# Column roll of an 8192 x 8192 float32 matrix: heads carried in four stages of 4 rows per partition, where it was two stages of 8 rows

## The chip, the core and the metric

The kernel runs on one core of a Trainium2 chip. The metric is the device time of one execution in microseconds (us), of which a lower one is better. Executions are called fast or slow by their state; all that are used here are fast, at a granted clock of 1.0. The experiments were run in groups, each called a call here; in the six calls, on at least four chips, the same kernel took from 818 to 833 us (817.75 and 821.00 us in two calls on one chip), so a time is only compared with the time of the kernel before in the same call.

A ratio is the mean time of one kernel's fast runs over that of the other's fast runs of the same rounds. It is not quite the ratio of the medians, which are quoted beside it. In the profile's lines DVE is VectorE, POOL the GpSimd engine, SP and ACT the two engines that issue the body copies; q0, q1 and q10 are DMA queues.

## The reference

```python
def setup_inputs():
    return {"x": np.random.randn(8192, 8192).astype(np.float32), "shift": 100}

def reference(x, shift):
    return np.roll(x, shift, axis=1)
```

Each row moves 100 columns to the right, and its last 100 columns come round to the front. Nothing is computed: 268.44 MB are read and 268.44 MB written.

## The kernel before

The output row is cut at column a = 128. The **body**, columns 128 and up, is copied from DRAM to DRAM, one row of 32256 bytes after another, on two hardware queues. The **heads**, columns 0 to 127 of every row, are gathered in SBUF, put together by VectorE, and stored from there by the software queue that POOL feeds. With s = 100 and g = a - s = 28, row r has a head of 100 columns from its own end and 28 columns from its own start. The rows are taken in groups of four (Q = 4). At each of the three borders inside a group, one load takes 128 columns across the border, the last 100 of one row and the first 28 of the next, and VectorE copies each part to its row's head. Only the 100 columns of the fourth row's own end and the 28 of the first row's own start are loaded by themselves.

```python
xm = x.rearrange("(c e j) w -> c j e w", e=16, j=4)
om = out.rearrange("(c e j) w -> c j e w", e=16, j=4)
for c in range(n_rows // 64):                      # the body
    for j in range(4):
        engines[j % 2].dma_start(out=om[c, j, :, a:], in_=xm[c, j, :, g:n_cols - s])
# ...
Q, J = 4, 8                                        # the heads
n_st = n_rows // (P * Q * J)                       # stages
reads = ctx.enter_context(tc.tile_pool(name="reads", bufs=n_st))
heads = ctx.enter_context(tc.tile_pool(name="heads", bufs=n_st))
# ... xt, ot: x and out as "(k p j q) c -> k q p j c"
for k in range(n_st):
    t = reads.tile([P, Q - 1, J, a], x.dtype)
    h = heads.tile([P, Q, J, a], x.dtype)
    for q in range(1, Q):
        lead = bass.AP(tensor=x.tensor, offset=(k * P * J * Q + q) * n_cols - s,
                       ap=[[J * Q * n_cols, P], [Q * n_cols, J], [1, a]])
        nc.gpsimd.dma_start(out=t[:, q - 1], in_=lead)
    nc.gpsimd.dma_start(out=h[:, Q - 1, :, :s], in_=xt[k, Q - 1, :, :, n_cols - s:])
    nc.vector.tensor_copy(h[:, :Q - 1, :, :s], t[:, :, :, :s])
    nc.gpsimd.dma_start(out=h[:, 0, :, s:], in_=xt[k, 0, :, :, :g])
    nc.vector.tensor_copy(h[:, 1:, :, s:], t[:, :, :, s:])
    tiles.append(h)
for k, h in enumerate(tiles):
    for q in range(Q):
        nc.gpsimd.dma_start(out=ot[k, q, :, :, :a], in_=h[:, q])
```

Of the kernel before, what the change touches and what calls it, by code (L numbers as in the profile page):

```python
# [1 line left out]

# [4 lines left out]


@with_exitstack
def kernel(  # L10
    ctx: ExitStack,
    tc: tile.TileContext,
    x: bass.AP,
    shift: int,
    out: bass.AP,
):
    nc = tc.nc
    n_rows, n_cols = x.shape
    s = shift % n_cols
    a = -(-s // 128) * 128  # L20
    g = a - s
    P = nc.NUM_PARTITIONS
    engines = [nc.sync, nc.scalar]
    n_chunks = 16
    rows = n_rows // n_chunks





    xm = x.rearrange("(c e j) w -> c j e w", e=16, j=4)
    om = out.rearrange("(c e j) w -> c j e w", e=16, j=4)
    if a < n_cols:
        for c in range(n_rows // 64):
            for j in range(4):
                engines[j % 2].dma_start(out=om[c, j, :, a:], in_=xm[c, j, :, g:n_cols - s])
    if a == 0:
        return


    if a > 512:
        for i in range(n_chunks):
            r = slice(i * rows, (i + 1) * rows)
            nc.gpsimd.dma_start(out=out[r, :s], in_=x[r, n_cols - s:])
            if g > 0:
                nc.gpsimd.dma_start(out=out[r, s:a], in_=x[r, :g])
        return





    Q, J = 4, 8
    n_st = n_rows // (P * Q * J)
    reads = ctx.enter_context(tc.tile_pool(name="reads", bufs=n_st))
    heads = ctx.enter_context(tc.tile_pool(name="heads", bufs=n_st))
    xt = x.rearrange("(k p j q) c -> k q p j c", q=Q, j=J, p=P)
    ot = out.rearrange("(k p j q) c -> k q p j c", q=Q, j=J, p=P)
    tiles = []
# [9 lines that stand above are left out]
        if g > 0:  # L69
# [8 lines that stand above are left out]
# [1 line left out]
_INS = ['x', 'shift']  # L79
_OUTS = [((8192, 8192), 'float32')]  # L80

_NUMBERS = {'shift': 100}


# [26 lines left out]
```

## Time and profile before

| | before |
|---|---|
| median of the first three runs | 828.16 us (828.02 to 828.73) |
| profiled execution | 826.9 us |
| DMA engines busy | all slices but the last |
| body queues q1 and q10 | 95.0% of the 16 engines' time |
| software queue q0 (heads) | 4.1% |
| heads over at | 252 us |

The page's slices, its queues, the waits of SP and a table by stretches are shown and read in the prediction. One more part of the page matters here, the DMA issues: output and input, issuing engine, number, KB of each, and the median us from issue to landing.

```profile
out_dram<-in_x_dram ACTq DMA_DIRECT2D x256, 504.0 KB, 12.7
out_dram<-in_x_dram SPq DMA_DIRECT2D x256, 504.0 KB, 12.7
out_dram<-h POOLq DMA_DIRECT2D x8, 512.0 KB, 97.6
```

A body copy of the same size as a head store lands in 12.7 us, a store in 97.6. The store isn't slow; it stands behind up to seven others on a queue that gets one small packet for each large one of the body.

### The profile page before, as it was taken

To read this page: it belongs to the slowest core of one execution; us is meant where nothing else is said; L and a number is where in the kernel's file an instruction comes from. 1 tells how busy PE (TensorE), PEld (TensorE's weight loads), DVE (VectorE), ACT (ScalarE), POOL (GpSimd) and SP (SyncE) were. 2 spreads that over 40 slices of the span, in tenths; PEclk is the share of its full clock that TensorE was granted. 3 is DMA by queue.
4 is the path that set the end of the run, shared out by engine and by line. 5 is a ranking of instruction groups with operands and counts; after the bars stand their busy time and mean duration, and the time that the engine had idled before them with its cause. 6 is when DMAs were issued, how large, how long until landed. Compare 5 with 4: busy or idle time off the path is not lost. (4 is left out here: it accounts for less than half of the span.)

```text
span 826.9 us, 589 instructions
## 1 busy us (share of the span) xinstructions
DVE 3.7 (0%) x4; POOL 16.1 (2%) x22
## 2 busy tenths in 40 slices
DVE  0000000000000000000000000000000000000000
POOL 3001001000000000000000000000000000000000
DMA  9999999999999999999999999999999999999997
GB/s 305 336 338 333 337 344 351 347 352 343 339 342 330 329 329 321 334 329 326 326 328 325 337 329 325 340 318 329 317 336 333 330 325 326 328 326 339 321 328 261
DMA packets 18724, 272.70 MB, mean 330 GB/s; under 512 B 8480, under 2 KB 8480, under 8 KB 10528
## 3 DMA queue, kind: packets, MB, share of 16 engines
q10 hardware_dynamic: 8192, 132.14, 47.8%
q1 hardware_dynamic: 8192, 132.14, 47.2%
q0 software_dynamic: 2336, 8.39, 4.1%
q14 instruction: 4, 0.03, 0.0%
HBM read 268.44 MB, written 268.44 MB: 649 GB/s over the span
## 5 line engine op out<-in xcount | busy, mean ns | idle before, releaser
L75 POOL DMA_DIRECT2D out_dram<-h x8 | 6.9, 955 | 92.4 <-DMA h<-in_x_dram 79.9
L66 POOL DMA_DIRECT2D t<-in_x_dram x6 | 5.4, 910 | 0.8 <-PEq L106 0.8
L68 DVE COPY h<-t 128x2400 f32<-128x2400 f32 x2 | 2.8, 1410 | 116.2 <-DMA t<-in_x_dram 116.2
L67 POOL DMA_DIRECT2D h<-in_x_dram x2 | 1.8, 882 | 15.1 <-DMA t<-in_x_dram 15.1
L70 POOL DMA_DIRECT2D h<-in_x_dram x2 | 1.8, 883 | 14.4 <-DMA t<-in_x_dram 14.4
L71 DVE COPY h<-t 128x672 f32<-128x672 f32 x2 | 1.0, 504 | 0.0
L92 POOL MEMSET const-float32-0.0<- 128x1 f32 x1 | 0.1, 98 | 0.2 <-issue 0.2
L92 POOL MEMSET const-bfloat16-1.0<- 128x1 bf16 x1 | 0.1, 101 | 0.0
L92 POOL MEMSET const-float32-1.0<- 128x1 f32 x1 | 0.1, 98 | 0.0
L92 POOL MEMSET const-uint8-127<- 128x1 uint8 x1 | 0.1, 98 | 0.0
## 6 DMA issues: line engine op xcount, KB each, us to landing
out_dram<-in_x_dram ACTq DMA_DIRECT2D x256, 504.0 KB, 12.7
out_dram<-in_x_dram SPq DMA_DIRECT2D x256, 504.0 KB, 12.7
out_dram<-h POOLq DMA_DIRECT2D x8, 512.0 KB, 97.6
t<-in_x_dram POOLq DMA_DIRECT2D x6, 512.0 KB, 65.8
h<-in_x_dram POOLq DMA_DIRECT2D x2, 400.0 KB, 84.0
h<-in_x_dram POOLq DMA_DIRECT2D x2, 112.0 KB, 81.3
```

The costliest lines, as they stand in the source:

```text
L66: nc.gpsimd.dma_start(out=t[:, q - 1], in_=lead)
L67: nc.gpsimd.dma_start(out=h[:, Q - 1, :, :s], in_=xt[k, Q - 1, :, :, n_cols - s:])
L68: nc.vector.tensor_copy(h[:, :Q - 1, :, :s], t[:, :, :, :s])
L70: nc.gpsimd.dma_start(out=h[:, 0, :, s:], in_=xt[k, 0, :, :, :g])
L71: nc.vector.tensor_copy(h[:, 1:, :, s:], t[:, :, :, s:])
L75: nc.gpsimd.dma_start(out=ot[k, q, :, :, :a], in_=h[:, q])
L92: nc = _bacc.Bacc("TRN2", target_bir_lowering=False, num_devices=1)
```

## The change

The intent is to have smaller stages: four instead of two, so that the first stores can start earlier and the transfers are finer. Nothing else is altered.

```diff
-    Q, J = 4, 8
+    Q, J = 4, 4
     n_st = n_rows // (P * Q * J)
```

Through n_st and J this makes 36 head DMAs of half the size out of 18, eight VectorE copies out of four, and a distance of 16 rows (512 KiB) in DRAM from one partition to the next, where it was 32 rows (1 MiB).

## The prediction

> **What bounds the kernel now.** I read the page's slices first, then its DMA queues, then the waits of the SP engine, then a table by stretches of time.
>
> ```profile
> span 826.9 us, 589 instructions
> DVE 3.7 (0%) x4; POOL 16.1 (2%) x22
> ...
> DMA  9999999999999999999999999999999999999997
> ...
> q10 hardware_dynamic: 8192, 132.14, 47.8%
> q1 hardware_dynamic: 8192, 132.14, 47.2%
> q0 software_dynamic: 2336, 8.39, 4.1%
> ...
> HBM read 268.44 MB, written 268.44 MB: 649 GB/s over the span
> ```
>
> The reader should see that no compute engine matters, and that the 16 DMA engines are busy in every slice but the last. The queue shares are time, and 47.8 + 47.2 + 4.1 = 99.1%: the DMA engines are the bound. Two hardware queues carry the body (columns 128 and up, straight from DRAM to DRAM), 264.28 MB; the software queue, fed by POOL, carries the heads (the first 128 output columns, through SBUF), 4.19 MB in and 4.19 MB out. The change touches q0 only.
>
> ```profile
> SPq L36 <- DMA out_dram<-in_x_dram: 679.2, 252, 6.0
> ```
>
> This is the longest wait of the SP sequencer: nearly always it waits for an earlier body copy to land before it may issue the next. So the body is refilled as fast as it drains, and if q0 uses an engine less, the body takes that time at once.
>
> ```profile
> 1.00:131.00 130.00, 3.66 (x4) 12.38 (x14) 1.00 0.99 335
> 131.00:252.00 121.00, 0.00 (x0) 3.47 (x4) 1.00 1.00 346
> 260.00:800.00 540.00, 0.00 (x0) 0.00 (x0) 1.00 1.00 328
> ```
>
> Columns: stretch, length, DVE, POOL, clock, share of the DMA engines, GB/s moved. From the trace's records of single packets, the tenth and last head load lands at 131 us and the eighth and last head store at 252 us; these three stretches are therefore loads, stores, and body alone. The heads are over with 575 us still to run. Nothing that makes the heads later by less than that can delay the end as a wait. They cost time only by the share of the 16 engines that they take.
>
> **What that share costs.** In the packet records body copies move 300.6 GB/s during the loads, 314.3 during the stores, and 328.1 alone. The loss is (328.1 - 300.6) x 131 us = 3.60 MB plus (328.1 - 314.3) x 121 us = 1.67 MB, together 5.27 MB, which at 328.1 GB/s is 16.1 us. This is the price of all the heads in the end time, 1.9% of it: 11.0 us for loads, 5.1 us for stores. It is less than the 33.9 us of q0 (4.1% of the span), because body packets take 1.39 us while loads run and 1.50 us while stores run, and 1.56 us alone; the small packets relieve them. If the heads became free the gain would be 2%, and to lose 2% they would have to double their price.
>
> **What the Trainium skill says.** "DMA: Bandwidth & Descriptors", section "Queues, rings and completion order": each engine goes round robin over the queues that have work, a packet at a time. The trace agrees in pace: a 512 KB store is eight data packets and one completion packet per engine, and eight stores took 121 us, 15.1 us each, so 1.68 us a turn, near one body packet of 1.50 us and one head packet of 0.17 us. Section "SWDGE vs HWDGE vs iDMA" of the same page puts a packet at preferably 4096 bytes and at most 64 descriptors. Here 1792 packets on q0 are 4096 bytes (eight rows of 512), 160 are 4400 (eleven rows of 400) and 32 are 4144 (37 of 112). Eleven and 37 are not multiples of the eight rows of a partition, so packets run across partitions, which the next part uses. Section "Rules for kernel authors" asks for at least 1 MiB a DMA; the trace contradicts that this matters here, since 0.5 MiB transfers with seven more behind them leave the engines at 1.00. Section "Latency and other measured facts" reports lower rates at partition pitches of large powers of two in HBM (207 GB/s at 512 KiB, 164 at 2 MiB); no run here has yet shown that, and it is a rival below.
>
> **The change part by part.** J goes from 8 to 4, so stages from 2 to 4. The SBUF held is the same (four stages of half the size), and so are the bytes and the rows of each descriptor.
> - *DMA instructions.* Loads 10 to 20, stores 8 to 16, each of half the size. POOL spends 0.88 to 0.96 us on each: 36 x 0.9 = 32 us instead of 16. It is spread over some 200 us, in which one DMA drains in about 8 us. Off the path: 0.
> - *Data packets.* A 256 KB transfer gives each engine 32 rows: four packets of eight. Loads of 400-byte rows give 11 + 11 + 10, three packets where 64 rows gave six; loads of 112-byte rows give one where 64 gave two. Sum: 2048 data packets before and after. Their time, 538.9 us in 16 engines, stays. 0.
> - *Completion packets.* One per DMA and engine: 288 becomes 576. The records give each 9 ns: 288 x 9 ns / 16 = 0.16 us. Even with a turn each they yield to the body, which loses nothing by it.
> - *Pace of the heads.* A completion packet takes a turn. Before: loads 6 x 9 + 2 x 7 + 2 x 3 = 74 turns in 131 us (1.77 us each), stores 8 x 9 = 72 in 121. After: loads 12 x 5 + 4 x 4 + 4 x 2 = 84 turns, 149 us; stores 16 x 5 = 80 turns, 134 us. So I expect the last load at about 149 us and the last store at about 283 us instead of 252. It lies beside the body and costs nothing.
> - *Waits for semaphores.* Before, the ninth head DMA was held 15.1 us although its tile was new: it waited for the first of the eight before it. So eight head DMAs may be in flight. After, eight of half the size are 40 turns, 67 us of work: q0 does not run dry. Median store latency should fall from 97.6 to about 67 us.
> - *DVE.* Eight copies instead of four, of half the size; 1410 ns becomes about 750 and 504 about 300. Total from 3.7 to about 4.2 us, off the path.
>
> Sum: +0.2 us on the path, in a kernel whose three runs lie 0.7 us apart.
>
> **Rivals.**
> 1. *Each DMA has a fixed price.* With 18 more at some 2 us of issue and landing each, 36 us would be added, to 864 us. Against: the heads end at 252 of 827 us and DMAs overlap, eight in flight.
> 2. *The software queue does not join the rows of two partitions.* With four rows per partition, packets of 512-byte rows would be 2048 bytes and there would be twice as many. If each costs half, nothing; if each keeps the 0.17 us of a store, 1792 x 0.17 / 16 = 19 us at the very worst of engine time, and about half of it (16.1/33.9) in the end time: 837 us. The 4400-byte packets speak against.
> 3. *The DRAM pitch from partition to partition falls from 1 MiB to 512 KiB.* Loads cost 0.35 us a packet on average where stores cost 0.17, though their lower half, too, takes 0.16: some loads meet congestion. If the new order of addresses removed all of it, loads would cost like stores and (11.0 - 5.1) = 6 us would go, to 822 us. Against: each transfer covers rows four apart without gap in both versions; only how many of them an engine takes in one piece changes. I expect at most 1 us.
> 4. *Completion packets stall an engine until its writes have landed.* 288 more, if each stopped its engine 1 us, would be 18 us, to 846. Against: the body has 8192 of them already and the engines' time is full with data packets.
>
> **Range and chances.** The sum gives 828.2 + 0.2, rival 3 draws a little down: 828.0 us. The range from 823.5 to 831.5 holds the spread of runs, another chip's small difference, most of rival 3 and a third of rival 2. Faster by 2% (under 811.6) needs all the heads free: 0.02. Slower by 2% (over 844.7) needs rival 1 or 4: 0.02. Within 2%: 0.96.
>
> **What would show it.** Right: DMA tenths at 9 up to the last slice; q0 with 2624 packets, 8.39 MB, about 4.1%; q1 and q10 unchanged; 36 head issues with stores landing in about 67 us; heads over at about 283 us; POOL near 32 us; the same 328 GB/s after the heads. Heads over by about 252 would mean that completion packets take no turn. Wrong: q0 with some 4400 packets (rival 2), load packets below 0.25 us on average (rival 3), body packets longer than 1.56 us or engines idle in the early slices (rival 4). A time off by 2% with none of these I could not explain.

## The result, and the profile after

The changed kernel took 832.34 us (median of 6 runs, 829.82 to 835.45), the kernel before 827.84 us (median of 6, 827.28 to 828.73). The ratio is 1.0055, with a 95% interval of 1.0034 to 1.0076. It is the same within 2%, as the prediction said, but 4.5 us slower and 0.8 us outside the stated range, and the interval leaves out 1. The profiled execution is the slowest of the six.

The page of the changed kernel, in the lines that answer to those of before:

```profile
span 833.3 us, 617 instructions
...
DVE 4.5 (1%) x8; POOL 27.2 (3%) x40
...
DMA  9999999999999999999999999999999999999997
...
q1 hardware_dynamic: 8192, 132.14, 47.7%
q10 hardware_dynamic: 8192, 132.14, 47.3%
q0 software_dynamic: 2624, 8.39, 4.0%
...
HBM read 268.44 MB, written 268.44 MB: 644 GB/s over the span
...
out_dram<-h POOLq DMA_DIRECT2D x16, 256.0 KB, 65.4
```

The queues carry the same bytes. q0 has 288 more packets, all of them completions, and no larger share. The engines are as busy as they were. So in this pair of executions nearly all of the additional time is not idle time of the engines: it must be in the duration of packets, and as q0's share did not grow, in those of the body. The wait of SP for body copies shows the same from the issuing side (679.2 us before).

```profile
SPq L36 <- DMA out_dram<-in_x_dram: 685.6, 252, 4.8
```

The table by stretches (stretch, length, DVE, POOL, clock, share of the DMA engines, GB/s), first of the kernel before:

```profile
60.00:125.00 65.00, 1.83 (x2) 3.46 (x4) 1.00 1.00 340
125.00:160.00 35.00, 0.00 (x0) 3.47 (x4) 1.00 1.00 349
160.00:284.00 124.00, 0.00 (x0) 0.00 (x0) 1.00 1.00 340
300.00:800.00 500.00, 0.00 (x0) 0.00 (x0) 1.00 1.00 328
```

and of the changed kernel:

```profile
60.00:125.00 65.00, 2.25 (x4) 6.90 (x9) 1.00 1.01 335
125.00:160.00 35.00, 1.03 (x2) 3.66 (x5) 1.00 1.00 322
160.00:284.00 124.00, 0.00 (x0) 5.68 (x8) 1.00 1.00 338
300.00:800.00 500.00, 0.00 (x0) 0.00 (x0) 1.00 1.00 327
```

The engines are at 1.00 in both, yet while the heads run they move fewer bytes, above all from 125 to 160 us, where loads give way to stores. In the records of single packets, 16 engines spend 786.6 us on the body instead of 780.7 us, and 33.3 us on the heads instead of 33.7. At 300 us the changed kernel is 44 body rows behind, which is 44 / 10.17 rows per us = 4.3 of the 6.4 us by which the two profiled executions differ.

A useful measure of this is the **relief**: how much shorter body packets are while heads run than when the body is alone, times their number, over 16 engines. Before: (1561 - 1443) ns x 2392 / 16 = 17.6 us. After: (1563 - 1489) ns x 2700 / 16 = 12.5 us. What the heads cost is their own 33.7 us less the relief, 16.1 us; in this execution of the changed kernel it is 33.3 - 12.5 = 20.8 us. The heads' own packets hardly changed, and the relief is 5 us smaller. These are two single executions, the second the slowest of six; the repeats further down show less of this.

### The profile page after: what moved, and what is told of

The parts are those of the page before. It is cut to its first block, busy times and chain, and to the rows that moved or that the text cites. A ratio compares the mean times of both kernels' runs of the same rounds, so it can differ in the third digit from the quotient of the medians.

```text
span 833.3 us, 617 instructions
## 1 busy us (share of the span) xinstructions
DVE 4.5 (1%) x8; POOL 27.2 (3%) x40
## 3 DMA queue, kind: packets, MB, share of 16 engines
q0 software_dynamic: 2624, 8.39, 4.0%
## 5 line engine op out<-in xcount | busy, mean ns | idle before, releaser
L75 POOL DMA_DIRECT2D out_dram<-h x16 | 11.6, 724 | 111.8 <-DMA out_dram<-h 59.8
L66 POOL DMA_DIRECT2D t<-in_x_dram x12 | 9.5, 792 | 34.6 <-DMA h<-in_x_dram 17.2
L68 DVE COPY h<-t 128x1200 f32<-128x1200 f32 x4 | 3.1, 786 | 141.6 <-DMA t<-in_x_dram 141.6
L67 POOL DMA_DIRECT2D h<-in_x_dram x4 | 3.0, 748 | 24.9 <-DMA t<-in_x_dram 24.9
L70 POOL DMA_DIRECT2D h<-in_x_dram x4 | 3.0, 748 | 24.0 <-DMA t<-in_x_dram 24.0
L71 DVE COPY h<-t 128x336 f32<-128x336 f32 x4 | 1.7, 425 | 0.0
## 6 DMA issues: line engine op xcount, KB each, us to landing
out_dram<-h POOLq DMA_DIRECT2D x16, 256.0 KB, 65.4
```

## The experiments

All kernels but one give the right result. Each was timed in 4 to 6 fast runs beside 9 to 11 runs of the kernel before in the same call.

### Is it the number of DMAs, their completions, or the order of rows in memory?

The stretches in which body packets grew suggested two theories: A, each further DMA stops its engines for some 0.3 us at its completion, or B, the new layout, four rows per partition, hurts. Cutting every head DMA in two without changing the layout separates them:

```diff
-            nc.gpsimd.dma_start(out=ot[k, q, :, :, :a], in_=h[:, q])
+            for j in (0, 4):
+                nc.gpsimd.dma_start(out=ot[k, q, :, j:j + 4, :a], in_=h[:, q, j:j + 4])
```

(and the loads in the same way).

> Two stages with 8 rows per partition as before, so the rows of DRAM go to the partitions as before, but every head DMA is cut in two over its rows: 36 DMAs, as many as in the changed kernel. Theory A (each further DMA has a price of its own, some 0.3 us per completion packet on each engine: 5.7 us more body packet time over 18 more completions): 832 us, 1.005 of before, heads over at about 284 us. Theory B (the order of the addresses, four rows per partition, costs the time): 828 us, 1.000 of before.

Measured: 819.95 us against 817.98 us before, ratio 1.0022 (1.0008 to 1.0035). It lies between the two expectations and decides nothing by itself. Its heads were over at 281 us, so the number of DMAs sets the pace of the heads whatever the layout is.

The completions by themselves:

```diff
+    pt = pings.tile([1, 144, 128], x.dtype)
+    for i in range(144):
+        nc.gpsimd.dma_start(out=pt[:, i], in_=x[i:i + 1, :128])
```

> The kernel before, with 144 further one-row loads of 512 bytes into a spare tile issued behind the heads, so that they fall into the stretch where the body runs alone. If each puts one completion packet on every engine, 2304 completions are added. Theory A (0.3 us of engine time for each): 144 x 0.3 = 43 us, 871 us. If a completion costs only its 9 ns: 144 x 9 ns = 1.3 us, 829 to 830 us.

Measured: 819.45 us against 817.98, ratio 1.002 (1.0008 to 1.0032): 1.6 us for 144 DMAs, where theory A asked for 43. The page and two stretches of this kernel:

```profile
q0 software_dynamic: 6944, 8.47, 4.4%
...
pt<-in_x_dram POOLq DMA_DIRECT2D x144, 0.5 KB, 24.7
```

```profile
252.00:690.00 438.00, 0.00 (x0) 66.30 (x137) 1.00 1.00 331
690.00:800.00 110.00, 0.00 (x0) 0.00 (x0) 1.00 1.00 333
```

q0 has 4608 packets more than the 2336 of before: on each engine 144 pieces of 32 bytes (a row of 512 bytes was spread over all 16) and 144 completions. The body next to them hardly loses, 331 GB/s against 333. A completion costs no more than about 1.6 us / 144 = 11 ns of engine time (5 to 18 ns by the interval, the piece of 32 bytes included), near the 9 ns that the records give. Theory A's price is excluded, and with it the prediction's rivals 1 and 4; these were loads, and for stores the run with 2 rows below says the same.

Then other sizes of stage, with the diff `Q, J = 4, 16` and `Q, J = 4, 2`.

> One stage with 16 rows per partition: 9 head DMAs instead of 18. Theory A: 9 x 0.3 us less, 825.3 us (0.997). Theory B: some change of either sign from the other address order, and the same number as A only by chance; stores start only when the whole load is done, so there can be a gap in the heads, which costs nothing.

Measured: 819.86 us against 817.98, ratio 1.0019 (1.0005 to 1.0033). Half the DMAs gained nothing.

> Eight stages with 2 rows per partition: 72 head DMAs, 54 more than before, packets still of 8 rows. Theory A: 54 x 0.3 = 16 us more, 844 us (1.020). Theory B: no fixed relation to the number of DMAs; if the step from 8 to 4 rows is the mechanism, one more halving gives perhaps as much again, 837 us (1.011).

Measured: 818.03 us against 817.98, ratio 1.0004 (0.9987 to 1.0021). 54 more DMAs of 128 KB and less cost nothing that these runs can see, and a step further in the direction of the change does not add to its loss. Both theories miss here: there is no rule by which fewer rows per partition are slower.

```profile
out_dram<-h POOLq DMA_DIRECT2D x32, 128.0 KB, 37.0
t<-in_x_dram POOLq DMA_DIRECT2D x24, 128.0 KB, 35.5
```

### Is it there at all?

With three of four kernels at 1.002, only one of them (the 144 small loads) where a completion's own 9 ns would put it, chance became a theory (C). The changed kernel was run twice more, unaltered, with a copy of the kernel before as a control.

> The changed kernel again, unaltered, beside the kernel before on the chip of this call. Theory B (the address order costs engine time): 1.005 of before again. Theory C (the 0.55% was chance: which of several equally good interleavings of the two body queues the runs of that call fell into): between 0.998 and 1.003.

Measured: 821.12 us against 818.13, ratio 1.0035 (1.0018 to 1.0051).

> The kernel before, unaltered, as if it were a new kernel. All theories: 1.000. What it differs from 1.000 by is what two identical programs differ by in this test; theory C expects up to 0.2 or 0.3%.

Measured: 817.43 us against 818.13, ratio 0.999 (0.9975 to 1.0006).

> The changed kernel a second time in the same call. Theory B: the same ratio as the first, near 1.005. Theory C: within 0.3% of 1, and not necessarily the same as the first.

Measured: 820.48 us against 818.13, ratio 1.0031 (1.001 to 1.0051). The loss is there on another chip, a little smaller: 2.7 us by the mean of the two ratios.

The body was run without any heads (a `return` ahead of them; a wrong result):

> The body alone, heads left out on purpose (columns 0 to 127 of the output are not written, so the result is wrong). The prediction's price for all head work, 16.1 us, should be missing: 828 - 16 = 812 us on a chip where before takes 828 us, or 818 - 16 = 802 us on one where it takes 818 us; ratio 0.980. If heads cost their whole engine time of 33.9 us, the ratio would be 0.959.

Measured: 801.7 us against 818.13, ratio 0.9797 (0.9782 to 0.9812), so the heads cost 818.13 x 0.0203 = 16.6 us. The page:

```profile
q10 hardware_dynamic: 8192, 132.14, 49.6%
q1 hardware_dynamic: 8192, 132.14, 49.5%
```

Two queues hold 99.1% of the engines' time, the same sum as three did before. This settles the price on which the prediction's chances rested: half of the heads' own engine time, not all of it.

### A price per transfer, or something that comes once?

If the loads or the stores of the changed kernel are dearer, repeating them makes it larger. The 512-byte loads were repeated four times into spare tiles, behind the stores, with 8 and with 4 rows:

```diff
+    again = ctx.enter_context(tc.tile_pool(name="again", bufs=4 * n_st))
+    for k in [k for _ in range(4) for k in range(n_st)]:
+        u = again.tile([P, Q - 1, J, a], x.dtype)
+        for q in range(1, Q):
+            nc.gpsimd.dma_start(out=u[:, q - 1], in_=lead)   # lead as above
```

> The kernel before with the three 512 KB loads of each stage issued four more times into spare tiles, behind the stores. The prediction priced all loads at 11.0 us, these are three quarters of them: four more sets cost 4 x 8.3 = 33 us, ratio 1.040. All theories say the same; it is the base for its sister with four rows per partition.

Measured: 843.55 us against 817.75, ratio 1.0322 (1.0305 to 1.034): 817.75 x 0.0322 / 4 = 6.6 us a set.

> The same with four rows per partition: four more sets of loads on top of the changed kernel. Theory D (the extra 2.7 us of the change lies in its loads): each set 2.0 us dearer, so 2.7 + 4 x 2.0 = 10.8 us over the sister with eight rows, 1.3% of the time. Theory E (it lies in the stores) or C (it comes once, from how the body queues fall in with the heads, and is not a price per transfer): 2.7 us or less over the sister.

Measured: 848.88 us (843.38 to 849.47) against 817.75, ratio 1.0368 (1.0341 to 1.0395). Over its sister: 817.75 x 0.0046 = 3.8 us, where theory D needed 10.8.

The stores three times more:

```diff
-    for k, h in enumerate(tiles):
+    for k, h in [kh for _ in range(4) for kh in enumerate(tiles)]:
```

> The kernel before with all stores of the heads issued three more times (the same bytes to the same place). The prediction priced all stores at 5.1 us: 3 x 5.1 = 15 us more, ratio 1.019.

Measured: 837.13 us against 817.75, ratio 1.0239 (1.0223 to 1.0255): 817.75 x 0.0239 / 3 = 6.5 us a set.

> The same with four rows per partition. Theory E (the extra 2.7 us of the change lies in its stores): 4 x 2.7 = 10.8 us over the sister with eight rows. Theory D or C: 2.7 us or less over the sister.

Measured: 840.52 us against 817.75, ratio 1.0284 (1.0262 to 1.0306): 817.75 x 0.0045 = 3.7 us over its sister, where theory E needed 10.8.

The loads of 400- and 112-byte rows, the only transfers not repeated so far, were repeated eight times:

```diff
+    for k in [k for _ in range(8) for k in range(n_st)]:
+        u = again.tile([P, J, a], x.dtype)
+        nc.gpsimd.dma_start(out=u[:, :, :s], in_=xt[k, Q - 1, :, :, n_cols - s:])
+        nc.gpsimd.dma_start(out=u[:, :, s:], in_=xt[k, 0, :, :, :g])
```

> The kernel before with the loads of 400- and 112-byte rows of each stage issued eight more times into spare tiles, behind the stores. They are a quarter of the loads by bytes, priced by the prediction at 11.0 x 0.25 = 2.8 us a set: 8 x 2.8 = 22 us more, ratio 1.027. It is the base for its sister.

Measured: 850.02 us against 832.55 (a slower chip), ratio 1.0217 (1.02 to 1.0234): 832.55 x 0.0217 / 8 = 2.3 us a set.

> The same with four rows per partition. Theory F (the 2.7 us or more of the change lie in these small-row loads): 9 x 2.7 = 24 us over the sister with eight rows. Theory C (it comes once, from the way heads and body interleave): 4 us or less over the sister.

Measured: 853.6 us against 832.55, ratio 1.0249 (1.023 to 1.0268): 832.55 x 0.0032 = 2.7 us over its sister, where theory F needed 24.

In all three pairs four rows lose some 3 us, as they do without repetition, although up to nine times the transfers are made. Theories D, E and F fall: the loss doesn't grow in proportion to the transfers. That it comes once, with the heads' first passage, is the reading that is left and is not shown. The spread of these pairs, 2 to 2.6 us with the intervals of both ratios, leaves room for up to about 1 us a set of 512-byte loads or of stores; the middle values are 0.3, 0.3 and 0 us.

### The order inside a stage

Theory C once more, as an accident of which transfers meet: the same transfers with q counted down instead of up, in loads and stores.

```diff
-        for q in range(1, Q):
+        for q in range(Q - 1, 0, -1):
# ...
-        for q in range(Q):
+        for q in range(Q - 1, -1, -1):
```

> The kernel before with the order of its 512-byte loads and of its stores within a stage turned round: the same transfers, the same number, the same bytes. A price of the transfers would give 1.000. Theory C (interleaving): up to 0.4% off, either way.

Measured: 831.26 us against 832.55, ratio 0.9982 (0.9968 to 0.9995).

> The changed kernel with the order turned round in the same way. If four rows per partition have an inherent price in the heads as a whole, 1.003 to 1.005 as before; theory C: anything between 0.999 and 1.005, and a value at 1.000 would speak for it.

Measured: 836.52 us against 832.55, ratio 1.0036 (1.0015 to 1.0056); over its sister 1.0036 / 0.9982 = 1.0054. The loss survives another order. Chance alone is no longer a good explanation: seven comparisons of four rows with eight (1.0055, 1.0035, 1.0031, and over their sisters 1.0045, 1.0044, 1.0031, 1.0054) have one sign, though some share a base. The stretches of the reversed kernels, eight rows first:

```profile
125.00:160.00 35.00, 0.00 (x0) 3.44 (x4) 1.00 1.00 346
160.00:290.00 130.00, 0.00 (x0) 0.00 (x0) 1.00 1.00 340
```

and four rows:

```profile
125.00:160.00 35.00, 1.20 (x2) 3.68 (x5) 1.00 1.01 329
160.00:290.00 130.00, 0.00 (x0) 5.68 (x8) 1.00 1.00 333
```

Again the rate falls from 125 us on, with the engines at 1.00. This led to theory G: the loss arises where head loads and head stores overlap. The repeats of the changed kernel already spoke against it: from 125 to 160 us they moved 343 and 351 GB/s, beside 349 in the copy of the kernel before, and were slower all the same.

### The passage from loads to stores

One kernel was to take the overlap away, by storing the last stage first; the other was to spread it over the heads, by storing each stage after the next one's loads.

```diff
-    for k, h in enumerate(tiles):
+    for k, h in list(enumerate(tiles))[::-1]:
```

> The changed kernel with the stages stored in reverse order, so the first store needs the last load: no head load and head store are in flight together. Theory G (the extra 3 us arise where head loads and head stores overlap, at the passage from one to the other): 1.000 of before, give or take 0.1%, and no stretch of long body packets at 125 to 155 us. If the passage is not the cause: 1.003 to 1.005 as the changed kernel.

Measured: 823.06 us against 821.0, ratio 1.0029 (1.0011 to 1.0047). The separation was only partly reached, as the timeline of POOL and DVE shows (start, us, engine, line, operation):

```profile
118.76 1.49 POOL L75 DMA_DIRECT2D out_dram<-h  x2 [20.44 <-DMA h<-in_x_dram]
142.68 0.79 DVE L68 COPY h<-t 128x1200 f32<-128x1200 f32 x1 [34.61 <-DMA t<-in_x_dram]
143.38 0.33 DVE L71 COPY h<-t 128x336 f32<-128x336 f32 x1
144.00 0.71 POOL L75 DMA_DIRECT2D out_dram<-h  x1 [23.75 <-DVE h L71]
```

Two stores were issued ahead of the last loads, at 118.76 us, against the order of the program; the others waited until 144 us. So two stores still overlapped with loads, where the changed kernel has five by 138 us. The loss stayed about what it was.

```diff
         tiles.append(h)
+        for m in ([k - 1] if k else []) + ([k] if k == n_st - 1 else []):
+            for q in range(Q):
+                nc.gpsimd.dma_start(out=ot[m, q, :, :, :a], in_=tiles[m][:, q])
-    for k, h in enumerate(tiles):
-        for q in range(Q):
-            nc.gpsimd.dma_start(out=ot[k, q, :, :, :a], in_=h[:, q])
```

> The changed kernel with each stage stored as soon as the next one's loads are issued: loads and stores overlap through most of the 280 us of the heads instead of some 25. Theory G: several times the extra, 1.010 or more. If overlap is not the cause: 1.003 to 1.005, or less.

Measured: 823.47 us against 821.0, ratio 1.0035 (1.002 to 1.005). The line of the stores and a piece of the timeline show that they did lie among the loads:

```profile
L75 POOL DMA_DIRECT2D out_dram<-h x16: 709/728/1027, 45.6 to 219.2; - x16
```

```profile
76.61 0.75 POOL L66 DMA_DIRECT2D t<-in_x_dram  x1 [6.93 <-DMA h<-in_x_dram]
79.92 0.75 POOL L67 DMA_DIRECT2D h<-in_x_dram  x1 [2.56 <-DMA h<-in_x_dram]
89.55 0.75 POOL L70 DMA_DIRECT2D h<-in_x_dram  x1 [8.88 <-DMA out_dram<-h]
96.59 0.74 POOL L75 DMA_DIRECT2D out_dram<-h  x1 [6.29 <-DMA out_dram<-h]
```

Stores begin at 45.6 us, and loads go on between them. An overlap several times as long costs no more, so theory G falls too.

### What the profiled executions have in common

The relief, worked out for each kernel whose head traffic is not repeated, from one execution each (us; "heads" is the heads' own time on 16 engines, "price" is heads less relief):

| kernel | rows per partition | head DMAs | heads | relief | price |
|---|---|---|---|---|---|
| before, its copy, reversed order | 8 | 18 | 33.7, 35.3, 33.5 | 17.6, 17.1, 17.0 | 16.1, 18.2, 16.5 |
| every DMA cut in two | 8 | 36 | 36.1 | 17.5 | 18.6 |
| changed kernel (three times) | 4 | 36 | 33.3, 34.1, 32.1 | 12.5, 15.0, 15.7 | 20.8, 19.1, 16.4 |
| reversed, last stage first, interleaved | 4 | 36 | 32.3, 32.7, 33.4 | 12.1, 14.3, 16.0 | 20.2, 18.4, 17.4 |
| 16 rows | 16 | 9 | 34.1 | 16.9 | 17.2 |
| 2 rows | 2 | 72 | 37.2 | 22.3 | 14.9 |

All six executions with four rows have less relief than all of those with eight, on the average 14.3 against 17.3 us, also where eight rows have 36 DMAs. But their own head packets are 1.7 us shorter on the average, so the price differs by only 1.4 us (18.7 against 17.3), and the two ranges overlap: 16.4 to 20.8 and 16.1 to 18.6. So the relief goes with the layout in these executions, and accounts for about half of a loss of some 3 us.

The second repeat of the changed kernel shows that it can't be the whole. Its span is 2.9 us longer than that of the copy of the kernel before, in the same call. Yet at 300 us it had moved 2901 body rows, the copy 2895, and its packets took only 0.4 us more on 16 engines in all (810.5 against 810.1 us). The rest was idle time of the engines, 8.2 against 5.7 us, most of it in the last 25 us of the span (4.9 against 3.0). This idle time is 5.7 to 9.0 us in the executions with eight rows and 6.5 to 10.0 in those with four, so it differs as much between executions of one layout as the loss is large. The decomposition of one execution is thus no surer than the loss that it is to explain.

## Why the prediction was right or wrong

- **The bound, and the price of the heads: right.** It put all head work at 16.1 us; taking the heads away gave 16.6. By parts it was rougher: a set of 512-byte loads 6.6 us instead of 8.3, the small-row loads 2.3 instead of 2.8, a set of stores 6.5 instead of 5.1. Dividing the loss by stretches of time gave the loads too much and the stores too little; the sum of the measured parts is 15.4. The body's 314.3 GB/s beside the stores is 312.8 when worked out again from the packet records, which makes the stores 5.6 us.
- **Packets and completions: right.** q0 has 2624 packets in 8.39 MB, packets do run across partitions, and a completion costs about 11 ns at most. The 2 us a DMA of rival 1 stand in no trace here.
- **The pace of the heads: right.** 283 us was expected for the last store; it landed at 287 us, and at 282 and 280 us in the repeats, where 252 would have meant no turn. Median store latency was 65.4 us for an expected 67. That a completion packet takes a turn of its own fits this, and fits another count: beside the 2336 packets of q0 some 2400 body rows were moved, beside the 2624 of the changed kernel 2700. One row for each packet of q0, although two queues carry the body, is what equal turns give if the body's completions, as many as its rows, take turns too.
- **POOL and DVE: right in place, off in size.** POOL took 27.2 us for an expected 32, as a DMA of half the rows needs 0.71 to 0.79 us instead of 0.88 to 0.96. DVE took 4.5 us for an expected 4.2. Neither is on the path.
- **"Sum: +0.2 us on the path": wrong, and this step failed.** Its term for data packets (their time "stays. 0") was right for the packets of the heads (33.7 us before, 33.3 after) and was taken for the whole effect. The same 16.1 us of heads had been worked out from body packets that get shorter beside them, and the sum took for granted that they would get shorter by as much with four rows and 36 DMAs. They did not: relief fell from 17.6 to 12.5 us in the first pair of executions, and from 17.1 to 15.0 and 15.7 us in the repeats. The sum's +0.2 us measured +4.5 us in the first call and +2.7 us in the second. The relief explains most of the first pair (a price of 20.8 instead of 16.1 us) and only part of the loss on the average; the rest stays open. The range followed the sum and left only 3.3 us for it.
- **Rival 3, the layout: named, but with the wrong sign for the end time.** It expected shorter load packets and a gain. The load packets did get a little shorter, 364 ns with eight rows and 340 with four (means of three and of four executions; 344 and 336 in the first pair). But what decided the first pair was the body, where the rival didn't look.
- **Chances: right.** With 16 us at stake, neither 2% was in reach of a change that leaves the heads in.

**What stays open.** The cause of the loss. What the runs exclude is a price of 0.3 us a completion, a price of a load or store that repeats in full with it, the order inside a stage (one other was tried), and the length of the overlap of loads and stores. They don't exclude the number of DMAs: with eight rows, 36 DMAs in place of 18 measured 1.0022 (1.0008 to 1.0035), and the unaltered repeats of the changed kernel, with 36 as well, 1.0035 and 1.0031, which these intervals don't tell apart. Against the number speaks only the run with 72 DMAs at 1.0004, which has another layout too. The test that would decide, the four-row layout with 18 DMAs, was not run; that each DMA would then need one dimension too many is the author's reason. Nor is it known why four rows gave less relief than eight, and two rows more. Part of the loss lies behind the heads: in the four pairs without repeated transfers the body alone ran 0.15 to 0.38% slower from 300 us to 800 us, 0.8 to 1.9 us, which no part of the change explains and which is of the size of the noise of a single execution.

No version here clearly beats the kernel before; reversed order with eight rows, at 0.9982, is as near to it as its own copy at 0.999.

## What to carry to other kernels

Where the DMA engines are full, price a stream by taking it out, and don't equate its price with its own busy time: here 34 us of packets cost 16.6 us, because the other stream ran faster beside them. The number and size of DMAs behind such a bound hardly mattered here as long as others of their queue were in flight, but "the same bytes" didn't mean "the same time" below half a per cent, and there only repeated runs beside the old kernel in the same call tell. A mechanism read off one profile should be looked for in a second profile of the same kernel, and doubled or removed, before it is believed; five plausible ones fell.

## What the Trainium skill lacked or had wrong

- "DMA: Bandwidth & Descriptors", section "Queues, rings and completion order", describes turns by packet, but not that the completion of a DMA takes a turn too. Counting it predicted the end of the heads at 283 us; it came at 287 (282 and 280 in the repeats), and at 281 where the DMAs were only cut in two.
- The same section calls 9 to 17 descriptors a typical packet. Here a packet of the hardware queues was one row of 32256 bytes, 1.44 to 1.56 us long on the average, against 4096 bytes and at best 0.16 us on the software queue. The traces don't show descriptors, so the number isn't refuted; but the turns are very unequal in bytes, which the page doesn't say.
- The same page's section "Rules for kernel authors" asks for 1 MiB a DMA and calls transfers below 64 KB mostly overhead. Behind a full body it cost nothing measurable to go from 512 KB to 128 KB (1.0004), and 144 DMAs of 512 bytes cost 1.6 us together. The fixed 2 us that its section "Anatomy of one DMA" gives each DMA, mostly completion latency by its own account, did not show as engine time: 144 of them would be 288 us.
- The page's only rates for copies between HBM tensors are those at large power-of-two row pitches, which the prediction quotes; no page has one for long rows one after another. With 32256-byte rows, one core alone, the traces show 327 to 333 GB/s, 660 GB/s of reading and writing together.
- No page says that a small stream shortens the packets of a large one beside it: body packets took 1.44 us beside heads and 1.56 us alone.
- No page warns of the difference between calls and chips at a bound of this kind: the same kernel had medians of 817.75 to 832.55 us in the six calls, on at least four chips, and of 817.75 and 821.00 us in two calls on one chip.
